# A scheduler rank 80 instructions ahead for the stages of neighbourhood attention and mLSTM

## The chip, the cores and the metric

The kernel runs on one core of a Trainium2 chip. The metric is device time in microseconds (us) of one launch, the median of several. TensorE does the matrix products and transposes, VectorE, ScalarE and GpSimd the arithmetic between them, and SyncE's queue issues the DMAs. In the profile they are PE (PEld is its weight load), DVE, ACT, POOL and SP.

## What is computed

Two models of two layers run one after the other on 512 tokens of 1024 features, in fp32. The first (two layers of sliding-window attention beside retention, then an MLP) takes up to about 1650 us and is not touched. The second has a context of 256 tokens beside x. Each of its layers, cut to what matters:

```python
h  = rmsnorm(x, g1) * (1 + sc1) + sh1          # adaLN: sh, sc, g from silu(c) @ w_ada
hc = the same for the context
p, pc = h @ w_in, hc @ w_in                    # q, k, v, o of mLSTM; q, k, v of attention; gates
# mLSTM, 8 heads of 64, both directions, context first, its end state begins x's scan
s   = (q @ k.T) * exp(b_t - b_s + i_s - m_t)
num = w_prev * (q @ C) + s @ v ;  den = w_prev * (q @ n) + sum(s)
y_m = head_layernorm(num / max(|den|, exp(-m_t))) * sigmoid(o)
# neighbourhood attention, 8 heads of 64, grid of 8 rows x 64 columns, 16 columns in sight
S   = [q @ k_window.T + bias + mask, q @ k_ctx.T]
y_n = softmax(S) @ [v_window, v_ctx]
x = x + g1 * ([y_m, y_n] @ w_out)
x = x + g2 * relu(modulated h @ w1)**2 @ w2    # the context too, but for the last layer
```

## The kernel before

Every large product is made of three fp32r products on TensorE: with a weight tile split in high and low parts (wh, wl) and the activation likewise, wh·xh, wh·xl, wl·xh (L241 to L243 where the weights are the loaded operand, L289 to L291 where they stream). Weights come by SyncE's DMA into wst (L215, 2 buffers); ScalarE makes whi (L225) and VectorE wlo (L226, the subtraction), 3 buffers each. PSUM has four tags: g with 3 buffers (products), s with 2 (scores), t with 2 (transposes, mLSTM states and outputs) and o with 1 (attention's values). SBUF tiles u come from one pool of 53.

*Neighbourhood attention of x* is na_x: 32 units, 8 heads by 4 blocks of 128 queries. Its stages: lead (once a head: key and query splits L405 to L422 on ScalarE and VectorE, 8 small bias DMAs L1286, 8 additions L1292 on GpSimd into btab); scores (products L1333 to L1339 into s; on VectorE the maxima L1341 and L1342, which adds the bias too, and the sign L1344; exp L1346 on ScalarE; then the division by the sum, L1220 and, by turns, L1222 on ScalarE or L1224 on VectorE); turn (transposes L1353 into t, copies L1355 and L1356); values (L1369 into o, every second head).

*mLSTM* is mlstm: 4 pairs of heads, each in steps of two chunks and two directions. Its stages: weights (row DMAs L1075, mask L1078 on GpSimd, exp L1081, and once a pair the turned keys, L1017 to L1023); prepare (row DMAs L1094, L1095 on VectorE, then the states: L1038 into t, VectorE's updates L1044); scores (L1106 into s, L1111 on VectorE); outs (L1118 and L1121 into t, the denominators L1123 to L1125, L1131 or L1134 on VectorE, the sum L1135 on GpSimd, and once a pair head_norm, L1159 to L1169); turn (L1145 into t, and a split L199 and L200).

Around them run the gate rows (scans L931 to L934 on VectorE), modulation for the next norms (products L824 into g, transposes L837 into t, sums L839 on VectorE), the rotations of q and k (L393 to L397, with swap DMAs L385) and the GEMMs. In order of time, second model: context mLSTM of layer 0 beside x's projections (1745 to 1870 us); x's attention beside more projections (to 2078); x's mLSTM beside the context's MLP (to 2300); x's MLP; then in layer 1 attention (2866 to 3014) and mLSTM (to 3200) beside what projections and modulation are left.

Two things set the order. First the program: generators are interleaved by mesh in proportion to their counts of steps, and within one, staged(n, *stages) runs in step i the stage d for unit i - d, deepest first, so that a stage that waits for another comes some steps later. Second, the scheduler below the program: it gives each instruction a rank, its place in the program, and lets each engine take next, of the instructions that are ready by its own reckoning, the one of lowest rank. Each engine then runs its list strictly as written. Buffers go round by tag in the order of the program.

Of the kernel before, what the change touches and what calls it, by code (L numbers as in the profile page):

```python
# [121 lines left out]
def staged(n, *stages):  # L122

    for i in range(n + len(stages) - 1):
        for d in reversed(range(len(stages))):
            if 0 <= i - d < n:
                stages[d](i - d)
        yield


def idle(i):
    pass


def chain(*gens):
# [14 lines left out]
class Net:  # L150
# [283 lines left out]
    def attention(self, zq, zk, av, sink8, ao):  # L434
# [57 lines left out]
        def values(i):  # L492
# [9 lines left out]
            if b == 3:  # L502
                ao.append(self.split(outs[p]))

        return staged(16, lead, idle, scores, idle, turn, idle, values)

    def retention(self, h, q, k, v, gate, rt):
# [72 lines left out]
    def first_block(self):  # L580
        nc, A = self.nc, self.A
        with self.pool("b1") as self.bp:
# [38 lines left out]

            nx, acc, hs = self.hybrid(0, acc, hs, gm, sink8[:, 0:8], chain([first], tiles), later)
            xs, acc, hs = self.hybrid(1, acc, hs, gm, sink8[:, 8:16], self.w_tiles(A["w_in"][1][:, 0:640], KT), idle)
        return xs, acc

# [177 lines left out]
    def modulation(self, l, i0, i1):  # L803
# [26 lines left out]
        def turn(i):  # L830
# [12 lines left out]
            if j in (3, 9):  # L843
# [4 lines left out]
                                               op0=ALU.add, op1=ALU.mult)  # L848

        return staged(i1 - i0, load, idle, work, turn)  # L850


# [201 lines left out]
    def mlstm(self, s, n, C, st, so, ys):  # L1054
# [7 lines left out]
        per = nch  # L1062
# [82 lines left out]
                nc.tensor.transpose(ps[:, 128 * c : 128 * c + 128], Hs[p][:, 128 * c : 128 * c + 128], self.ident)  # L1145
            ys.append(self.split(ps[:, :n], n))

        return staged(4 * per, weights, prepare, scores, idle, outs, idle, idle, turn)

    def head_norm(self, H, p, so, n):  # L1150

# [144 lines left out]
    def na_x(self, l, zq, zk, V, zkc, vc, ys):  # L1296

        nc = self.nc
        mm = nc.tensor.matmul
        grid = lambda ap: ap.rearrange("p (r c) -> p r c", c=64)  # L1300

        def perm(ap, out):
            if out:
                return ap.rearrange("p (b r c) -> p r b c", b=4, r=8)
            return ap.rearrange("p (r b c) -> p r b c", r=8, b=4)

        def patch(ap, v0, v1):

            ap = grid(ap)
            if v1 < 3:  # L1310
                return [(256, ap[:, :, 16 * v0 + 8 : 16 * v0 + 40].rearrange("p r (j c) -> p j r c", j=2))]
            outer = bass.AP(ap.tensor, ap.offset, [ap.ap[0], [56, 2], [64, 8], [1, 8]])
            return [(128, ap[:, :, 16 * v0 + 8 : 16 * v0 + 24]), (128, outer)]


        blocks = [(0, 0, 3), (256, 0, 1), (256, 1, 2), (512, 2, 3)]
        heads, outs, units = {}, {}, {}

        def lead(i):
            h, b = divmod(i, 4)  # L1320
            if b:
                return
            p, p0 = h // 2, 64 * (h % 2)
            heads[h] = (self.key_pairs(zk[p], p0, T), self.key_pairs(zkc[p], p0, 256),
                        self.query_stack(zq[p], p0, T, perm), self.bias_table(l, h))

        def scores(i):
            h, b = divmod(i, 4)
            o, v0, v1 = blocks[b]
            (kh, kl), (ch, cl), qs, tb = heads[h]  # L1330
            S = self.ps("s")
            lq = qs[:, 128 * b : 128 * b + 128]
            mm(out=S[:, 0:256], lhsT=lq, rhs=ch, start=True, stop=False)  # L1333
            mm(out=S[:, 0:256], lhsT=lq, rhs=cl, start=False, stop=True)
            mx, den = [self.t(self.bp, [128, 2], F32, tag, 4) for tag in ("nmx", "nden")]
            c = 256
            for (n, hi), (_, lo) in zip(patch(kh, v0, v1), patch(kl, v0, v1)):
                mm(out=S[:, c : c + n], lhsT=lq, rhs=hi, start=True, stop=False)
                mm(out=S[:, c : c + n], lhsT=lq, rhs=lo, start=False, stop=True)  # L1339
                c += n  # L1340
            nc.vector.tensor_reduce(mx[:, 0:1], S[:, 0:256], axis=AX.X, op=ALU.max)  # L1341
            nc.vector.tensor_tensor_reduce(S[:, 256:512], S[:, 256:512], tb[:, o : o + 256], 1.0, mx[:, 0:1],  # L1342
                                           ALU.add, ALU.max, mx[:, 1:2])
            nc.vector.tensor_scalar(mx[:, 1:2], mx[:, 1:2], -1.0, None, op0=ALU.mult)  # L1344
            P = units[i] = self.u()
            nc.scalar.activation(P, S, AF.Exp, bias=mx[:, 1:2], accum_out=den[:, 0:1])  # L1346
            self.na_scale(P, den[:, 0:1], i % 2)

        def turn(i):
            P = units[i]  # L1350
            pt = self.ps("t")
            for c in range(4):
                nc.tensor.transpose(pt[:, 128 * c : 128 * c + 128], P[:, 128 * c : 128 * c + 128], self.ident)  # L1353
            PT = units[i] = self.u()
            nc.scalar.activation(PT[:, 0:224], pt[:, 0:224], AF.Copy)  # L1355
            nc.vector.tensor_copy(PT[:, 224:512], pt[:, 224:512])  # L1356

        def values(i):
            h, b = divmod(i, 4)
            if h % 2 == 0:  # L1360
                return
            p = h // 2
            if b == 0:
                outs[p] = self.ps("o")
            PT = [units.pop(i - 4), units.pop(i)]
            _, v0, v1 = blocks[b]
            for c, v in enumerate((vc[0], vc[1], V[v0], V[v1])):
                for j in range(2):
                    mm(out=outs[p][64 * j : 64 * j + 64, 128 * b : 128 * b + 128],  # L1369
                       lhsT=v[:, 128 * p + 64 * j : 128 * p + 64 * j + 64], rhs=PT[j][:, 128 * c : 128 * c + 128],  # L1370
                       start=c == 0, stop=c == 3)
            if b == 3:
                self.na_finish(outs[p], T, perm, ys)

        return staged(32, lead, idle, idle, idle, idle, scores, idle, turn, idle, values)

    def na_values(self, w, hs, V, c0):

# [256 lines left out]
```

## Time and profile before

| | us |
|---|---|
| median of 3 runs | 3564.49 (3561.7 to 3566.58) |
| the profiled execution | 3575.06 |
| its span in the profile | 3573.3 |
| TensorE busy | 3437.6 (96%) |
| VectorE, ScalarE, GpSimd busy | 2023.8, 1444.9, 391.1 |

Busy time is that of one profiled execution, which took 10.6 us more than the median. TensorE's matmuls overlap and their ends are modelled, so 96% busy is not 96% of its peak; what TensorE waits for is read from its gaps and from the granted clock of a stretch.

### The profile page before, as it was taken

How to read it: one execution, taken by the hardware profiler on the slowest of the kernel's cores; microseconds unless marked ns; L12 is line 12 of the kernel's file. 1: busy time of each engine (PE TensorE's matmuls, PEld its weight loads, DVE VectorE, ACT ScalarE, POOL GpSimd, SP SyncE). 2: the span in 40 equal slices, each digit the busy share in tenths (PEclk: the TensorE clock that was granted, in tenths of full speed). 3: DMA queues.
4: the chain of work that ended last, by engine and by line, in shares of the span. 5: the costliest groups of instructions: out<-in, count | busy, mean ns of one | idle time of the engine just before them, and what ended most of it. 6: DMA issues, size and time to landing. Idle time of an engine off the chain costs nothing.

```text
span 3573.3 us, 48619 instructions
## 1 busy us (share of the span) xinstructions
PE 3437.6 (96%) x18835; PEld 2851.7 (80%) x18835; DVE 2023.8 (57%) x3791; ACT 1444.9 (40%) x2458; POOL 391.1 (11%) x512
## 2 busy tenths in 40 slices
PE   8999999999999999999998999999999999899998
PEld 7878888888778888787777788888888877668886
DVE  5654454455654454557657668764445577574444
ACT  4533332234532332335634664443334356333233
POOL 2120000001020010001112222100000122310000
PEclk9999999999999999999999999999999999899999
DMA  5322323334422432236645445533234334523322
GB/s 171 104 68 83 124 94 100 100 112 137 133 65 83 135 118 95 95 98 205 209 130 149 108 137 160 168 118 95 95 103 128 98 117 127 168 95 106 94 94 71
DMA packets 397655, 419.12 MB, mean 117 GB/s; under 512 B 38064, under 2 KB 343152, under 8 KB 397040
## 3 DMA queue, kind: packets, MB, share of 16 engines
q1 hardware_dynamic: 397424, 416.00, 37.4%
q8 instruction: 149, 2.44, 0.3%
q14 instruction: 82, 0.67, 0.1%
HBM read 391.55 MB, written 13.37 MB: 113 GB/s over the span
## 4 chain that ended last, share of the span: by engine, by line
PE 78%; DVE 9%; DMA 5%; ACT 3%; issue 3%; POOL 1%; SPq 1%; DVEq 0%; ACTq 0%; POOLq 0%
PE g L241 22%; PE g L242 22%; PE g L243 22%; DVE wlo L226 2%; PE g L289 1%; PE g L290 1%; PE g L824 1%; DMA u<-t 1%; PE g L291 1%; DMA u<-u 1%; ACT whi L225 1%; PE t L524 1%; DMA wst<-in_w_mlp 1%; PE o L1369 1%; POOL u L396 1%
## 5 line engine op out<-in xcount | busy, mean ns | idle before, releaser
L241 PE MATMUL g<-u,whi 128*128 128x512 f32 (+1 forms) x3680 | 1412.0, 384 | 9.5 <-ACT whi L225 3.1
L242 PE MATMUL g<-u,whi 128*128 128x512 f32 (+1 forms) x3680 | 1407.3, 383 | 4.9 <-DVE u L200 3.5
L243 PE MATMUL g<-u,wlo 128*128 128x512 f32 (+1 forms) x3680 | 1405.9, 382 | 3.4 <-DVE wlo L226 3.3
L225 ACT ACTIVATE whi<-wst 128x1024 fp32r<-128x1024 f32 (+1 forms) x628 | 621.7, 993 | 1352.2 <-PE g L242 1124.0
L226 DVE TENSOR_TENSOR wlo<-wst,whi 128x1024 fp32r<-128x1024 f32 (+1 forms) x628 | 729.0, 1164 | 425.4 <-ACT whi L225 417.7
L241 PEld LDWEIGHTS g<-u,whi 128*128 128x128 f32 x3680 | 694.8, 189 | 157.3 <-ACT whi L225 8.2
L242 PEld LDWEIGHTS g<-u,whi 128*128 128x128 f32 x3680 | 695.9, 189 | 138.3 <-DVE u L200 4.1
L243 PEld LDWEIGHTS g<-u,wlo 128*128 128x128 f32 x3680 | 694.9, 189 | 137.3 <-DVE wlo L226 5.5
L199 ACT ACTIVATE u<-u 128x512 fp32r<-128x512 f32 (+1 forms) x200 | 119.4, 597 | 289.7 <-DVE u L574 202.3
L200 DVE TENSOR_TENSOR u<-u,u 128x512 fp32r<-128x512 f32 (+1 forms) x200 | 132.9, 665 | 101.7 <-ACT u L199 100.9
L1485 DVE SCALAR_TENSOR_TENSOR u<-g,t,u 128x256 f32<-128x256 f32 (+1 forms) x128 | 78.1, 615 | 195.0 <-PE g L243 194.6
L289 PE MATMUL g<-whi,u 128*128 128x256 f32 (+1 forms) x576 | 167.9, 292 | 3.0 <-ACT rv L667 1.9
L291 PE MATMUL g<-whi,u 128*128 128x256 f32 (+1 forms) x576 | 164.6, 286 | 0.0
L290 PE MATMUL g<-wlo,u 128*128 128x256 f32 (+1 forms) x576 | 164.3, 286 | 0.0
L241 PE MATMUL g<-hc,whi 128*128 128x256 f32 x464 | 133.6, 290 | 6.9 <-ACT whi L225 5.1
L243 PE MATMUL g<-hc,wlo 128*128 128x256 f32 x464 | 132.0, 287 | 3.6 <-DVE wlo L226 3.6
L731 DVE TENSOR_TENSOR u<-g,u 128x512 f32<-128x512 f32 x64 | 44.3, 691 | 154.0 <-PE g L243 154.0
L242 PE MATMUL g<-hc,whi 128*128 128x256 f32 x464 | 131.3, 285 | 0.0
L868 POOL TENSOR_TENSOR u<-u,u 128x512 f32<-128x512 f32 (+1 forms) x28 | 35.7, 1274 | 864.4 <-ACT u L865 559.2
L289 PEld LDWEIGHTS g<-whi,u 128*128 128x128 f32 x576 | 110.7, 192 | 16.8 <-issue 7.7
L291 PEld LDWEIGHTS g<-whi,u 128*128 128x128 f32 x576 | 111.5, 193 | 1.2 <-issue 1.2
L290 PEld LDWEIGHTS g<-wlo,u 128*128 128x128 f32 x576 | 111.2, 193 | 1.1 <-issue 0.9
(302 smaller groups left out, 4055.4 us busy)
## 6 DMA issues: line engine op xcount, KB each, us to landing
wst<-in_w_mlp SPq DMA_DIRECT2D x96, 1024.0 KB, 5.4
wst<-in_w_in SPq DMA_DIRECT2D x60, 1024.0 KB, 5.4
u<-in_w_ada SPq DMA_DIRECT2D x192, 256.0 KB, 5.1
wst<-in_w_in SPq DMA_DIRECT2D x72, 512.0 KB, 4.0
wst<-in_w_up SPq DMA_DIRECT2D x32, 1024.0 KB, 5.5
wst<-in_w_down SPq DMA_DIRECT2D x32, 1024.0 KB, 5.2
wst<-in_w_out SPq DMA_DIRECT2D x20, 1024.0 KB, 5.4
u<-t SPq DMA_DIRECT2D x128, 128.0 KB, 5.2
```

The source lines that it names most:

```text
L199: nc.scalar.activation(hi, src, AF.Copy)
L200: nc.vector.tensor_tensor(lo, src, hi.bitcast(F32), op=ALU.subtract)
L225: nc.scalar.activation(h, v, AF.Copy)
L226: nc.vector.tensor_tensor(l, v, h.bitcast(F32), op=ALU.subtract)
L241: mm(out=ps, lhsT=wh, rhs=xh, start=first, stop=False)
L242: mm(out=ps, lhsT=wh, rhs=xl, start=False, stop=False)
L243: mm(out=ps, lhsT=wl, rhs=xh, start=False, stop=last)
L289: mm(out=ps, lhsT=xs[k][0][:, bs], rhs=wh[:, kk], start=k == 0, stop=False)
L290: mm(out=ps, lhsT=xs[k][0][:, bs], rhs=wl[:, kk], start=False, stop=False)
L291: mm(out=ps, lhsT=xs[k][1][:, bs], rhs=wh[:, kk], start=False, stop=k == KT - 1)
L731: nc.vector.tensor_tensor(t, ps, r2, op=ALU.mult)
L1485: V.scalar_tensor_tensor(xs[m], ps, mod[:, 40 + m, c : c + 1], xs[m], op0=ALU.mult, op1=ALU.add)
```

## The change

A helper, urgent, wraps the stages of mlstm and of na_x, so that whatever a stage emits gets a rank 80 places ahead of its place in the program. Idle stages stay as they are. The state-only mLSTM of the last layer's context (mlstm_states), the context's attention (na_ctx), GEMMs, gate rows, rotations and modulation are not wrapped. The order in which a stage takes its buffers is that of the program, as before. Each engine has the same instructions as before, in another order.

```diff
+def urgent(tc, ahead, *stages):
+
+    def wrap(f):
+        def g(i):
+            with tc.high_priority(ahead):
+                f(i)
+        return idle if f is idle else g
+    return [wrap(f) for f in stages]
...
-        return staged(4 * per, weights, prepare, scores, idle, outs, idle, idle, turn)
+        return staged(4 * per, *urgent(self.tc, 80, weights, prepare, scores, idle, outs, idle, idle, turn))
...
-        return staged(32, lead, idle, idle, idle, idle, scores, idle, turn, idle, values)
+        return staged(32, *urgent(self.tc, 80, lead, idle, idle, idle, idle, scores, idle, turn, idle, values))
```

The helper takes ten lines, so below it a line of the changed kernel has a number higher by 10: L1342 of before is L1352 there. A name such as s_2928 is a tile with its running number, the same in both.

VectorE in attention of layer 0, about 1936 to 1943 us in the trace, where s_2928 and s_2934 are the scores of two successive blocks, nmx their maxima, and u_2918 and u_2919 are gate rows. Before:

```order
L422 TENSOR_TENSOR u_2907_15776<-u_2772_15001,u_2907_15776 64x8x4x16
L931 SCALAR_TENSOR_TENSOR u_2918_15837<-u_2842_15456,mend_2411_13302,u_2841_15454 8x512
L932 SCALAR_TENSOR_TENSOR u_2918_15837<-u_2842_15456,mend_2411_13302,u_2841_15454 8x512
L1342 ISA s_2928_15868,nmx_2929_15871<-s_2928_15868,btab_2868_15583,nmx_2929_15871 128x256
L1342 ISA nmx_2929_15871 128x1
L933 SCALAR_TENSOR_TENSOR u_2919_15838<-u_2920_15841,u_2842_15456 8x512
L934 SCALAR_TENSOR_TENSOR u_2919_15838<-u_2920_15841,u_2842_15456 8x512
L1356 COPY u_2927_15865<-t_2926_15860 128x288
L1344 TENSOR_SCALAR nmx_2929_15871<-nmx_2929_15871 128x1
L1341 TENSOR_REDUCE nmx_2935_15895<-s_2934_15892 128x1
```

And changed:

```order
L1351 TENSOR_REDUCE nmx_2929_15871<-s_2928_15868 128x1
L1351 TENSOR_REDUCE nmx_2935_15895<-s_2934_15892 128x1
L1352 ISA s_2928_15868,nmx_2929_15871<-s_2928_15868,btab_2868_15583,nmx_2929_15871 128x256
L1352 ISA nmx_2929_15871 128x1
L1352 ISA s_2934_15892,nmx_2935_15895<-s_2934_15892,btab_2868_15583,nmx_2935_15895 128x256
L1352 ISA nmx_2935_15895 128x1
L1354 TENSOR_SCALAR nmx_2929_15871<-nmx_2929_15871 128x1
L405 TENSOR_TENSOR u_2890_15709<-u_2890_15709,u_2847_15466 128x512
L1354 TENSOR_SCALAR nmx_2935_15895<-nmx_2935_15895 128x1
L941 SCALAR_TENSOR_TENSOR u_2918_15837<-u_2842_15456,mend_2411_13302,u_2841_15454 8x512
L407 TENSOR_TENSOR u_2890_15709<-u_2890_15709,u_2891_15710 128x512
L942 SCALAR_TENSOR_TENSOR u_2918_15837<-u_2842_15456,mend_2411_13302,u_2841_15454 8x512
```

Both maxima, their bias additions and the sign of the first (L1344, now L1354) stand ahead of the gate scans and of the rotation L395 and L397 of u_2890 (now L405 and L407), which earlier stood ahead of L422 and after the first maximum.

TensorE at the same place, the scores s_2941 of the next block, before:

```order
L291 MATMUL g_2993_16194<-whi_2988_16184,u_2279_12684 128x256
L289 MATMUL g_2993_16194<-whi_2988_16184,u_2282_12716 128x256
L1333 MATMUL s_2941_15940<-u_2865_15566,u_2866_15571 128x256
L1334 MATMUL s_2941_15940<-u_2865_15566,u_2866_15571 128x256
L1338 MATMUL s_2941_15940<-u_2863_15560,u_2866_15571 128x256
L1339 MATMUL s_2941_15940<-u_2864_15561,u_2866_15571 128x256
L290 MATMUL g_2993_16194<-wlo_2989_16185,u_2282_12716 128x256
L291 MATMUL g_2993_16194<-whi_2988_16184,u_2283_12717 128x256
L289 MATMUL g_2993_16194<-whi_2988_16184,u_2290_12736 128x256
L290 MATMUL g_2993_16194<-wlo_2989_16185,u_2290_12736 128x256
L291 MATMUL g_2993_16194<-whi_2988_16184,u_2291_12737 128x256
L289 MATMUL g_2993_16194<-whi_2988_16184,u_2298_12776 128x256
```

And changed, up to the transposes t_2939 that need the first block's probabilities u_2931:

```order
L300 MATMUL g_2974_16096<-wlo_2913_15802,u_2298_12776 128x256
L1343 MATMUL s_2941_15940<-u_2865_15566,u_2866_15571 128x256
L1344 MATMUL s_2941_15940<-u_2865_15566,u_2866_15571 128x256
L1348 MATMUL s_2941_15940<-u_2863_15560,u_2866_15571 128x256
L1349 MATMUL s_2941_15940<-u_2864_15561,u_2866_15571 128x256
L301 MATMUL g_2974_16096<-whi_2912_15801,u_2299_12777 128x256
L299 MATMUL g_2974_16096<-whi_2915_15807,u_2301_12783 128x256
L300 MATMUL g_2974_16096<-wlo_2916_15808,u_2301_12783 128x256
L301 MATMUL g_2974_16096<-whi_2915_15807,u_2302_12784 128x256
L1343 MATMUL s_2952_16001<-u_2865_15566,u_2866_15571 128x256
L1344 MATMUL s_2952_16001<-u_2865_15566,u_2866_15571 128x256
L1363 MATMUL t_2939_15932<-t_35_36_104,u_2931_15880 128x128 x4
```

The scores now stand among the products of g_2974, which earlier were all ahead of them, and t_2939 follows after 4 more products and 2 of the scores of s_2952; before, it followed 8 products behind s_2941.

VectorE in the context mLSTM of layer 0, where t_2653 and t_2673 are outputs in PSUM, t_2665 and t_2666 sums for the states, and u_2655 the output that frees t_2653. Before:

```order
L1123 SCALAR_TENSOR_TENSOR mden_2654_14401<-t_2653_14394,gcols_2474_13555 128x4
L1044 SCALAR_TENSOR_TENSOR t_2209_2210_12343<-t_2209_2210_12343,wc_2480_13577,t_2665_14446 64x65
L1124 TENSOR_TENSOR mden_2654_14401<-mden_2654_14401,t_2653_14394 128x4
L1044 SCALAR_TENSOR_TENSOR t_2209_2210_12343<-t_2209_2210_12343,wc_2480_13577,t_2665_14446 64x65
L1125 RECIPROCAL mden_2654_14401<-mden_2654_14401 128x4
L1044 SCALAR_TENSOR_TENSOR C_2588_14061<-t_2209_2210_12343,wc_2480_13577,t_2665_14446 64x65 x2
L1134 TENSOR_TENSOR u_2655_14405<-t_2653_14394,mden_2654_14401 128x256
L1044 SCALAR_TENSOR_TENSOR t_2209_2210_12343<-t_2209_2210_12343,wc_2480_13577,t_2666_14457 64x65
```

And changed, the rows up to the same u_2655:

```order
L1054 SCALAR_TENSOR_TENSOR C_2588_14061<-t_2209_2210_12343,wc_2480_13577,t_2666_14457 64x65 x2
L236 TENSOR_TENSOR wlo_2670_14477<-wst_2668_14474,whi_2669_14476 128x1024
L1133 SCALAR_TENSOR_TENSOR mden_2674_14516<-t_2673_14509,gcols_2474_13555 128x4
L236 TENSOR_TENSOR wlo_2691_14570<-wst_2668_14474,whi_2690_14569 128x1024
L1134 TENSOR_TENSOR mden_2674_14516<-mden_2674_14516,t_2673_14509 128x4
L1135 RECIPROCAL mden_2674_14516<-mden_2674_14516 128x4
L236 TENSOR_TENSOR wlo_2720_14726<-wst_2718_14723,whi_2719_14725 128x1024
L1144 TENSOR_TENSOR u_2655_14405<-t_2653_14394,mden_2654_14401 128x256
```

Three weight splits (L226, now L236) and the denominators of the next output t_2673 came between the denominators of t_2653 and u_2655.

## Rows read from the trace of the kernel before

**Rows 1.** the page's head and first part: busy time of each engine
```profile
span 3573.3 us, 48619 instructions
...
PE 3437.6 (96%) x18835; PEld 2851.7 (80%) x18835; DVE 2023.8 (57%) x3791; ACT 1444.9 (40%) x2458; POOL 391.1 (11%) x512
```

**Rows 2.** stretches A:B: length, then busy us (instructions) by engine, PE clock granted
```profile
1745.00:1870.00 125.00, 121.28 (x746) 94.98 (x746) 69.22 (x204) 52.91 (x104) 26.80 (x46) 0.97 0.51 161
1870.00:2078.00 208.00, 190.20 (x1348) 158.80 (x1348) 145.33 (x342) 119.62 (x230) 54.34 (x95) 0.95 0.43 121
2078.00:2300.00 222.00, 204.73 (x1735) 195.45 (x1732) 185.54 (x434) 113.34 (x231) 52.42 (x67) 0.96 0.52 159
2866.00:3014.00 148.00, 138.86 (x939) 113.11 (x938) 119.33 (x282) 83.14 (x175) 37.86 (x60) 0.99 0.39 112
3014.00:3200.00 186.00, 163.02 (x1022) 119.18 (x1021) 114.74 (x318) 75.32 (x152) 47.79 (x62) 0.88 0.47 149
sum 889.00, PE 818.09 PEld 681.52 DVE 634.16 ACT 444.33 POOL 219.20; mean PE 163.62 PEld 136.30 DVE 126.83 ACT 88.87 POOL 43.84
```

**Rows 3.** what ended TensorE's waits, 1870 to 2078: us, times, longest
```profile
PE t L1353 <- DVE u L1224: 5.4, 3, 2.3
PE s L1333 <- ACT u L1346: 4.5, 2, 4.2
...
PE t L1353 <- ACT u L1222: 2.1, 2, 1.7
```

**Rows 4.** TensorE in order of time: start, us, [idle before <-what ended it]
```profile
1939.69 0.28 PE L291 MATMUL g<-whi,u 128*128 128x256 f32 x1
1939.80 0.28 PE L289 MATMUL g<-whi,u 128*128 128x256 f32 x1
1944.30 0.58 PE L1333 MATMUL s<-u,u 128*128 128x256 f32 x1 [4.22 <-ACT u L1346]
```

**Rows 5.** ScalarE in order of time, the exp before those scores
```profile
1943.47 0.69 ACT L1346 ACTIVATE u<-s,nmx 128x512 f32<-128x512 f32 x1 [4.11 <-DVE nmx L1344]
```

**Rows 6.** VectorE in order of time, the same place
```profile
1934.33 0.69 DVE L397 TENSOR_TENSOR u<-u,u 128x512 f32<-128x512 f32 x1 [1.74 <-POOL u L396]
...
1937.22 1.27 DVE L931 TENSOR_TENSOR_SCAN u<-u,mend,u 8x512 f32<-8x512 f32 x1
...
1939.81 0.49 DVE L1342 CUSTOM_DVE_ANT_0 s<-s,btab,nmx 128x256 f32<-128x256 f32 x1
...
1941.55 1.21 DVE L934 TENSOR_TENSOR_SCAN u<-u,u 8x512 f32<-8x512 f32 x1
...
1943.28 0.15 DVE L1344 TENSOR_SCALAR nmx<-nmx 128x1 f32<-128x1 f32 x1
```

**Rows 7.** two half-clock stretches, columns as in rows 2
```profile
1941.00:1947.80 6.80, 3.50 (x17) 3.50 (x17) 6.59 (x20) 2.08 (x6) 0.09 (x1) 0.61 0.48 155
3099.00:3115.00 16.00, 13.69 (x39) 7.30 (x38) 9.12 (x27) 2.76 (x7) 0.23 (x1) 0.52 0.26 78
```

**Rows 8.** VectorE's larger weight splits, 2078 to 2300: count, busy us, mean ns
```profile
L226 DVE TENSOR_TENSOR wlo<-wst,whi 128x1024 fp32r<-128x1024 f32 x27 | 32.7, 1219 | 14.1 <-ACT whi L225 13.9 <-issue 0.3
```

**Rows 9.** what ended TensorE's waits, 1745 to 1870
```profile
PE t L1038 <- DVE u L1134: 2.3, 1, 2.3
```

**Rows 10.** what ended TensorE's waits, 2078 to 2300
```profile
PE g L243 <- DVE wlo L226: 5.3, 6, 1.7
```

**Rows 11.** line L226 alone, 2078 to 2300: count, ns min/median/max
```profile
L226 DVE TENSOR_TENSOR wlo<-wst,whi x81: 677/693/1759, 2077.0 to 2299.2; 128x512 fp32r<-128x512 f32 x54, 128x1024 fp32r<-128x1024 f32 x27
```

**Rows 12.** what ended TensorE's waits, 2866 to 3014
```profile
PE s L1333 <- ACT u L1346: 2.2, 2, 2.0
...
PE o L1369 <- DVE u L1356: 1.4, 2, 1.2
```

**Rows 13.** what ended TensorE's waits, 3014 to 3175
```profile
PE t L837 <- DVE u L1356: 3.4, 1, 3.4
```

**Rows 14.** what ended the waits of SyncE's queue, 1745 to 2300
```profile
SPq L215 <- DVE wlo L226: 112.5, 18, 16.9
```

## The prediction

> **What bounds the kernel now.** I read the page first: TensorE is busy 3437.6 of 3573.3 us, 96% [rows 1]. Nothing but its own work, its waits and its clock can move the end by much, and the change takes no work away: each engine keeps every instruction that it had. So I went to TensorE's idle and half-clock time. The order is the same on every engine up to about 1750 us of the span, and nearly the same between 2300 and 2866 us, where only x's MLP runs; neither part can change by itself. The table by stretches [rows 2] gives the rest: 889 us in which TensorE is busy 818, so 71 us are idle (about 65 of them in gaps over 0.15 us). The granted clock there is 0.88 to 0.99 of full, which is a few stretches at half speed (1.2 GHz for 2.4) among full-speed ones. These two stocks, 71 us of idling and the half-clock time, are all that a new order can gain from. What it can lose is not bounded so: it can make new waits.
>
> Then I asked for each of these stretches what ended TensorE's waits, and laid out the work queued on each engine in the old and the new order, each instruction with its own duration from the trace; "earlier by 5 us" below means that so much less work stands ahead of it on its own engine.
>
> **The change, part by part.** In these five stretches a stage of attention or mLSTM moves ahead of up to 80 instructions (over all engines) of the surrounding GEMMs, of modulation and of the gate arithmetic. Nothing is added.
>
> *Attention, layer 0 (1870 to 2078 us).* TensorE waits 4.5 us for exp, 5.4 us for the scaled probabilities (L1224) and 2.1 us for those of ScalarE (L1222) [rows 3]. The largest single wait is 4.22 us, for scores s_2941 [rows 4]. It needs the s buffer that exp frees; exp waited 4.11 us for the negated maximum L1344 [rows 5]; and on VectorE the maximum L1342 of that block stands behind L397 with its 1.74 us wait and two gate scans, and L1344 behind two scans more [rows 6]. Scans L931 to L934 take 1.27, 1.27, 1.21 and 1.21 us. With L397 (0.69 + 1.74) that is 7.4 us of queue; the new order puts all of it behind L1344, and the next block's L1341 and L1342 (some 0.9 us) ahead: exp can start about 6.5 us sooner. TensorE also comes to s_2941 sooner, as 13 of the 24 products of g_2974 that stood ahead go behind it, at 0.11 us each (the step between rows at full clock [rows 4]), 1.4 us. That wait nearly vanishes. But next come the transposes L1353 t_2939, which need P after L1224, and on VectorE the delayed work now stands there: L395 (0.7, as L397), L397, L931, L932, two copies L1356 and L1224 (0.5 each) and two small ones, 5.6 us after the L1344 in question. Exp (0.7 [rows 5] and 0.2 to read its sum), scores and the 4 products left between them give TensorE about 2.3 us of that. So about 3.3 us of the 4.2 come back as a wait of L1353 for L1224, and with its remainder at s_2941 I take 0 for this place. Bounds: the whole 4.2 us goes, and the half-clock stretch after it (3.50 us busy at 0.61 [rows 7], so 3.50 x 0.39 = 1.4 us), -5.6; the scans cost a second such wait, +3. Near 2012 us, transposes t_3130, which waited 1.7 us for L1222, get 23 products ahead, 23 x 0.11 = 2.5 us, which covers them: -1.7 (0 to -1.7). The other attention scores there move up by 1 to 2 us, transposes by none, so L1224's 5.4 us stand, neither gain nor loss.
>
> *Context mLSTM, layer 0 (1745 to 1870 us).* Scores come 5 to 7 us earlier on TensorE, outs 4 to 6 us; both had 9 us and more to spare in the trace, so that is worth nothing by itself. The t tag of PSUM has two buffers, and states (L1038) and outs (L1118) take them in turn; L1134 frees the one of outs. In the old order VectorE reaches L1134 of u_2655 right behind the reciprocal and two state updates. In the new one three weight splits of 128x1024 stand ahead (1.22 us each [rows 8]), with products L1123 that wait for TensorE. The one L1038 that waited for L1134 paid 2.3 us [rows 9]. By the queues, two more states and one outs now come 4.6 to 7 us before their buffer is free, of which the GEMM products behind cannot help, since TensorE takes its work in order; part is the same wait seen three times. I take one and a half waits of the old size more: +3.5 (0 to +7).
>
> *mLSTM of x, layer 0 (2078 to 2300 us).* Scores move up 10 us and outs 6 us, from 18 us and more of slack: 0. What is passed is the weight splits L226, 1.4 us later at the median and up to 9.9. TensorE's products by wlo already wait for them 6 times, 5.3 us [rows 10]: here there is no slack, VectorE being busy 186 of 222 us [rows 2]. With three wlo buffers most of the delay is absorbed; I take half the old wait again: +2.5 (-2 to +8: the longest of them gone at one end; at the other each doubled, and 3 us for a half-clock stretch).
>
> One rule speaks against the change in these first three stretches. VectorE's splits meet GpSimd work: of 81 splits the median takes 0.69 us and the longest 1.76 [rows 11]. The Trainium skill, page "SBUF — State Buffer", section "Summary: rules for kernel authors", says that a VectorE operation with two SBUF inputs and a GpSimd operation that reads SBUF exclude each other, the later one blocking until the first ends. The slow splits of this trace agree with that, though no run here isolates it. By it, if GpSimd's bias and state work drawn forward met each of the six waiting splits, at 0.5 us each, the sum would be some 3 us higher, 3568.
>
> *Attention, layer 1 (2866 to 3014 us).* The same change of scans against L1342. TensorE waits 2.2 us for exp and 1.4 us for copies L1356 [rows 12], both behind scans. Scores move up 3 us and their products by V 4 us, with producers that hardly move. Of the 3.6 us I take half away: -2 (-5 with the other short waits, +3 if the lead of 3 us becomes a wait).
>
> *mLSTM of x, layer 1 (3014 to 3200 us).* Here TensorE is busy 163 of 186 at 0.88 [rows 2], the worst stretch; 3099 to 3115 alone lost 13.69 x 0.48 = 6.6 us to the clock [rows 7], and L837 waits 3.4 us for a t buffer that L1356 frees [rows 13]. But little GEMM work is left to overtake, the shifts are 0 to 3 us, and the chain of t buffers stays: -2 (-8, that clock and half of that wait; +4, one more such wait).
>
> *SyncE's queue.* Bias loads (8 per head) and row loads L1075 go ahead of some weight loads and swaps L385. Weight loads L215 stood waiting for a split to free their buffer, 18 times, 112.5 us [rows 14], so a place in the queue is not what sets them: 0, at most +3 (half of the mean wait of 6 us, once).
>
> Sum: 0 - 1.7 + 3.5 + 2.5 - 2 - 2 + 0 = +0.3 us on the profiled run's 3575.06 us. That run is 10.6 us above the median 3564.49, 1.8 us of it outside the span; I put the sum on the median: 3564.8. The ends added up are -22 and +28, but they are not one event.
>
> **The rivals.** *A, faster: GEMM work saved becomes filler.* The products passed over are still there when the latency chains at the end of each stretch run dry, so later gaps and half-clock stretches close as well. For it: the scores move by more than their waits. Against it: the transposes, the next link, don't move. If half of 12.0 us [rows 3], 3.6 [rows 12], 3.4 [rows 13] and 1.4 + 6.6 of clock [rows 7] go, that is 13.5 us, and no new waits come: 3551. All of it would be 3537.
>
> *B, slower: weight splits come late.* Attention and mLSTM fill VectorE ahead of L226, and TensorE stands at the third product of a tile with nothing behind that it may do first. For it: the six waits without slack; against it: three buffers. With context +7, mLSTM +8, L1353 +3 and the gains -5: +13, 3577. It decides from the point where the delay of a split (median 1.4 us) exceeds what its buffers hold in hand.
>
> *C: the order changes and the time of no wait does*, because TensorE reaches its data later than it is made, or the producers on ScalarE and VectorE set each step: 3564.5. It lies inside my forecast, and I count it there.
>
> **How the numbers follow.** About 0.2%, 7 us, is what a measurement of this kernel can tell from no change, so 3557.4 to 3571.6 is "the same". Forecast with C 0.46, spread 3556 to 3572: 0.42 inside, 0.04 below. A 0.29, faster. B 0.25, slower. Faster 0.33, same 0.42, slower 0.25. A reaches down to 3537 and B to about 3583; of each I leave out the far third, 0.17 in all: 3545 to 3578. The forecast's own range is 3556 to 3572.
>
> **What would show it.** Right: the 4.2 us wait of L1333 for exp is gone and a wait of L1353 for L1224 or L1220 of 2 to 4 us stands near it; L1038 and L1118 wait in all 3 to 7 us between 1745 and 1870; waits of L243 for wlo rise from 5.3 to about 8 us in the mLSTM of layer 0; the stretch up to 1745 us is as long as before. Wrong towards A: idle time over the affected stretches falls below 60 us, the clock in the tail above 0.92. Wrong towards B: L243 for wlo above 12 us, new half-clock stretches between 2078 and 2300.

## The result and the profile after

| | before | after |
|---|---|---|
| median, us | 3565.53 (4 runs, 3561.7 to 3568.41) | 3594.31 (4 runs, 3590.1 to 3599.64) |
| profiled execution, us | 3575.06 | 3593.33 |
| its span, us | 3573.3 | 3591.5 |
| TensorE busy, us | 3437.6 | 3463.2 |

The ratio of after to before is 1.0074, with a 95% interval of 1.0055 to 1.0093: the change costs about 27 us. The prediction was 3564.8 with a range of 3545 to 3578, so it was wrong. The profiled run of before stood 10 us above its median and that of after at its median, so the two traces show only 18 us of the difference.

The head of the page after:

```profile
span 3591.5 us, 48655 instructions
...
PE 3463.2 (96%) x18835; PEld 2853.2 (79%) x18835; DVE 2024.0 (56%) x3791; ACT 1443.9 (40%) x2458; POOL 385.4 (11%) x512
```

Against [rows 1], TensorE is busy 25.6 us longer with the same 18835 products; VectorE and ScalarE work as long as before, GpSimd 5.7 us less. The table by stretches, with the columns of [rows 2], each stretch moved by what the work had slipped at its ends:

```profile
1745.00:1869.00 124.00, 122.62 (x747) 93.82 (x746) 68.42 (x205) 53.43 (x104) 26.67 (x46) 1.00 0.52 163
1869.00:2080.00 211.00, 199.03 (x1345) 158.46 (x1344) 146.46 (x342) 118.61 (x229) 50.43 (x94) 0.96 0.44 124
2080.00:2310.00 230.00, 211.57 (x1707) 198.73 (x1706) 179.84 (x427) 110.41 (x228) 51.11 (x67) 0.95 0.51 154
2876.00:3034.00 158.00, 148.60 (x931) 114.27 (x931) 116.90 (x280) 81.95 (x172) 36.45 (x60) 0.99 0.36 103
3034.00:3218.00 184.00, 162.72 (x1023) 118.88 (x1022) 116.67 (x316) 76.69 (x155) 48.52 (x62) 0.91 0.49 152
sum 907.00, PE 844.55 PEld 684.15 DVE 628.29 ACT 441.10 POOL 213.18; mean PE 168.91 PEld 136.83 DVE 125.66 ACT 88.22 POOL 42.64
```

The reading takes two subtractions. Idle time of TensorE *fell*, from 889 - 818 = 71 us to 907 - 844.6 = 62 us. The granted clock of TensorE is no worse in sum (0.97 to 1.00 in the first stretch, 0.96 to 0.95 in the third, 0.88 to 0.91 in the last). Both stocks that the prediction watched moved the right way, and yet the stretches take 18 us longer, because TensorE's own work grew by 26.5 us. Attention of layer 0 (208 to 211 us), mLSTM of layer 0 (222 to 230) and attention of layer 1 (148 to 158) lost; the context mLSTM (125 to 124) and the last mLSTM (186 to 184) did not.

Which products grew is seen when the page's groups are asked for by line, from 1745 us to the end of the affected part. The columns are busy us and mean ns of one, then idle time before. Before:

```profile
L1369 PE MATMUL o<-u,u 128*64 128x128 f32 x256 | 30.7, 292 | 1.4 <-DVE u L1356 1.4
...
L1369 PE MATMUL o<-u,hc 128*64 128x128 f32 x256 | 23.8, 275 | 0.0
...
L1106 PE MATMUL s<-u,u 64*128 64x128 f32 x160 | 22.0, 335 | 1.0 <-DVE u L1111 0.5 <-ACT u L1346 0.5
```

And after:

```profile
L1379 PE MATMUL o<-u,u 128*64 128x128 f32 x256 | 43.4, 300 | 3.8 <-DVE u L1366 2.2 <-DVE u L1225 1.4 <-ACT u L1365 0.2
...
L1379 PE MATMUL o<-u,hc 128*64 128x128 f32 x256 | 32.9, 294 | 0.0
...
L1116 PE MATMUL s<-u,u 64*128 64x128 f32 x160 | 30.2, 339 | 2.1 <-DVE u L1121 1.1 <-ACT u L1356 1.0
```

Attention's values grew from 54.5 to 76.3 us and mLSTM's scores from 22.0 to 30.2, at nearly the same mean per product. Busy time counts the time in which at least one product of the group runs, so the products that share this time have become fewer: many that ran two at a time before run one at a time now. Both groups use half of the array: 128*64 is 64 columns (the two heads of a pair beside each other), 64*128 is 64 rows. The order in time shows how. TensorE before, one block of values (columns: start, us, line):

```profile
2004.38 0.66 PE L1369 MATMUL o<-u,u 128*64 128x128 f32 x8
2004.87 0.61 PE L1369 MATMUL o<-u,hc 128*64 128x128 f32 x8
```

Eight products (an fp32 product leaves two records) run through in 1.1 us. TensorE after, two score products of one block, then a block of values of the same kind as above:

```profile
1960.31 0.28 PE L1348 MATMUL s<-u,u 128*128 128x256 f32 x1
1960.43 0.29 PE L1349 MATMUL s<-u,u 128*128 128x256 f32 x1
...
1961.68 0.38 PE L1343 MATMUL s<-u,u 128*128 128x256 f32 x1
1961.99 0.43 PE L1379 MATMUL o<-u,u 128*64 128x128 f32 x2
1962.35 0.66 PE L1363 MATMUL t<-t,u 128*128 128x128 f32 x4
1962.94 0.43 PE L1379 MATMUL o<-u,u 128*64 128x128 f32 x2
1963.30 0.39 PE L1344 MATMUL s<-u,u 128*128 128x256 f32 x1
1963.62 0.43 PE L1379 MATMUL o<-u,u 128*64 128x128 f32 x2
1963.98 0.33 PE L1348 MATMUL s<-u,u 128*128 128x128 f32 x1
```

Single value products stand between single score products and transposes. From start to start a lone value product takes 0.36 us (1961.99 to 1962.35) and a score product 0.31 (1961.68 to 1961.99), where a score product inside its own block steps by 0.12 (1960.31 to 1960.43). Nothing waits here: the rows carry no idle time. The order pieces ahead of the prediction showed scores among GEMM products, but not this.

### The profile page after: what moved, and what is told of

Read it like the earlier page. It is cut to its first block, busy times and chain, and to the rows that moved or that the text cites. A ratio compares the mean times of both kernels' runs of the same rounds, so it can differ in the third digit from the quotient of the medians.

```text
span 3591.5 us, 48655 instructions
## 1 busy us (share of the span) xinstructions
PE 3463.2 (96%) x18835; PEld 2853.2 (79%) x18835; DVE 2024.0 (56%) x3791; ACT 1443.9 (40%) x2458; POOL 385.4 (11%) x512
## 4 chain that ended last, share of the span: by engine, by line
PE 81%; DVE 9%; ACT 3%; DMA 3%; issue 2%; POOL 1%; SPq 1%; DVEq 0%; POOLq 0%; ACTq 0%
PE g L251 22%; PE g L253 22%; PE g L252 22%; DVE wlo L236 2%; PE g L299 1%; PE g L300 1%; PE g L301 1%; PE g L834 1%; PE o L1379 1%; DMA u<-u 1%; PE t L534 1%; ACT whi L235 1%; PE t L1131 1%; PE t L1363 1%; POOL u L406 1%
## 5 line engine op out<-in xcount | busy, mean ns | idle before, releaser
L253 PE MATMUL g<-u,wlo 128*128 128x512 f32 (+1 forms) x3680 | 1405.7, 383 | 4.2 <-DVE wlo L236 3.7
L236 DVE TENSOR_TENSOR wlo<-wst,whi 128x1024 fp32r<-128x1024 f32 (+1 forms) x628 | 725.7, 1158 | 430.9 <-ACT whi L235 423.1
L253 PEld LDWEIGHTS g<-u,wlo 128*128 128x128 f32 x3680 | 693.2, 189 | 139.6 <-DVE wlo L236 7.1
L253 PE MATMUL g<-hc,wlo 128*128 128x256 f32 x464 | 133.0, 289 | 0.6 <-DVE wlo L236 0.5
```

The source lines that it names most:

```text
L236: nc.vector.tensor_tensor(l, v, h.bitcast(F32), op=ALU.subtract)
L253: mm(out=ps, lhsT=wl, rhs=xh, start=False, stop=last)
```

## The experiments

Two theories were open at first. **S**: TensorE pays for a change between fp32 products and fp32r products (fp32r is the format of the large products). **B**, the prediction's rival: weight splits come late on VectorE. S was replaced by **T** after price, ahead20, ahead160 and glue_after: TensorE pays for a change between products on the full array and on half of it, and a half-array product without its partner runs alone. The counts are taken from the program's order on TensorE, over the whole kernel. A change is counted wherever one product and the next use different shapes of the array: 128x128, 64 columns, 64 rows, or the 32 columns of modulation's products (L824); the expectations call all of these changes between full-array and half-array products. A product on part of the array is alone when neither neighbour uses the same shape at another place of the array.

| kernel | changes of shape | alone | ratio to before, 95% interval | median, us |
|---|---|---|---|---|
| before | 432 | 92 | | 3565 to 3570 |
| after | 591 | 163 | 1.0074 (1.0055 to 1.0093) | 3594.3 |
| ahead20 | 758 | 271 | 1.0151 (1.0134 to 1.0168) | 3618.1 |
| ahead160 | 570 | 163 | 1.0110 (1.0095 to 1.0125) | 3605.2 |
| glue_after | 486 | 110 | 1.0047 (1.0032 to 1.0062) | 3583.5 |
| rev_after | 385 | 84 | 0.9980 (0.9970 to 0.9991) | 3561.8 |
| vrev_before | 387 | 72 | 0.9957 (0.9943 to 0.9970) | 3553.4 |
| na_only | 539 | 120 | 1.0029 (1.0014 to 1.0043) | 3573.3 |
| ml_only | 464 | 127 | 1.0033 (1.0022 to 1.0044) | 3578.1 |
| rev_before | 374 | 69 | 0.9953 (0.9937 to 0.9968) | 3549.5 |
| few_changes | 284 | 54 | 0.9948 (0.9928 to 0.9968) | 3547.4 |

The kernels were timed in groups, each beside its own runs of before: to glue_after (3565.4; after itself 3565.5), rev_after and vrev_before (3570.1), and the rest (3565.3). Between groups the ratios are to be compared, not the medians.

**price: what a change of number format costs.** The added products, at the end:

```diff
+        for i in range(96):
+            mm(out=g[:, 0:256], lhsT=r[:, 128:256], rhs=r[:, 0:256], start=True, stop=True)
+        for i in range(96):
+            mm(out=t[:, 0:128], lhsT=f[:, 128:256], rhs=f[:, 0:128], start=True, stop=True)
+        for i in range(96):
+            one_r(i)
+            one_f(i)
```

> The kernel before with 864 products added behind its last output, which no output depends on: 192 fp32r products of 128x256 (192 in a row, the first 96 to warm the clock), 96 fp32 products of 128x128 in a row, then 96 of each by turns, then 24 times four of one and four of the other, then 96 fp32r again. Theory S (TensorE pays for each change between fp32 and fp32r products): from the trace of before and after, a change there and back costs about 0.22 us, so the part by turns takes 96 x 0.22 = 21 us longer than the two rows of 96 together, the part by fours 24 x 0.22 = 5 us longer. Rival B (nothing is paid for a change, the loss comes from weight splits that come late): both parts take as long as the two rows together, within 1 us.

TensorE in order of time, the two rows of 96 and the first rounds by turns:

```profile
3573.48 11.68 PE L794 MATMUL g<-u 128*128 128x256 f32 x96
3585.01 21.60 PE L796 MATMUL t<-u 128*128 128x128 f32 x192
3606.36 0.36 PE L786 MATMUL g<-u 128*128 128x256 f32 x1
3606.57 0.38 PE L789 MATMUL t<-u 128*128 128x128 f32 x2
3606.70 0.36 PE L786 MATMUL g<-u 128*128 128x256 f32 x1
```

In rows, an fp32r product takes 11.5 / 96 = 0.12 us and an fp32 product 21.4 / 96 = 0.22. By turns a round takes 0.34 (3606.36 to 3606.70), the sum of the two. A change of format costs nothing, and by fours neither (24 rounds from 3639.00 to 3671.80, 32.8 us). S falls.

**ahead20, ahead160, glue_after.** The first two change one number, in both return lines; the third keeps a block's products together:

```diff
-        return staged(32, *urgent(self.tc, 80, lead, ...
+        return staged(32, *urgent(self.tc, 20, lead, ...
```

```diff
+    def glue(self, on):
+        import contextlib
+        return self.tc.high_priority(2000) if on else contextlib.nullcontext()
...
             for c, v in enumerate((vc[0], vc[1], V[v0], V[v1])):
                 for j in range(2):
-                    mm(out=outs[p][64 * j : 64 * j + 64, ...
+                    with self.glue(c or j):
+                        mm(out=outs[p][64 * j : 64 * j + 64, ...
```

> The change with 20 in place of 80. Changes between fp32 and fp32r products on TensorE, counted in the order: 744 before, 960 with 80, 1258 with 20. Weight splits on VectorE stand 0.4 us later in the mean in the mLSTM of layer 0, against 2.2 with 80. Theory S (each change costs about 0.11 us): 514 changes more than before, +57 us, 3622, some 30 us slower than with 80. Rival B (late weight splits): the delay is a fifth of that with 80, so between before and after, 3566 to 3575.

> The change with 160 in place of 80. Changes between fp32 and fp32r products: 932 (960 with 80). Weight splits in the mLSTM of layer 0 2.8 us later in the mean (2.2 with 80). Theory S: 188 changes more than before, +21 us, 3587, a little faster than with 80. Rival B: slower than with 80, about 3600.

> The change as it is, but in each stage the products on TensorE after the first of a block (scores, transposes, outs, states, values) get a rank 2000 places ahead, so that a block that has begun is not cut up. Changes between fp32 and fp32r products: 804 (744 before, 960 after). Weight splits in the mLSTM of layer 0 stand 2.5 us later in the mean (2.2 after): VectorE's order is that of after. Theory S: 60 changes more than before, +7 us, 3572. Rival B: as after, 3594 or more.

ahead20 came to 3618.1 (S said 3622, B at most 3575): with hardly any delay of the weight splits (0.4 us in the mean) it is the worst of all, so B can't be the main cause. Its rows by line, columns as above:

```profile
L1379 PE MATMUL o<-u,u 128*64 128x128 f32 x256 | 45.7, 298 | 0.7 <-DVE u L1366 0.4 <-ACT u L1365 0.2
L1379 PE MATMUL o<-u,hc 128*64 128x128 f32 x256 | 37.8, 291 | 0.0
L1048 PE MATMUL t<-vw,u 128*64 128x65 f32 x384 | 34.9, 243 | 1.8 <-DVE hrs L327 1.7
```

The states L1038 (L1048 here), 18.4 us before, are the third group on half of the array, and now they are cut as well. glue_after missed S's 3572 by 11 us and was 11 us better than after: keeping blocks whole helped by less than hoped, because it did not keep the values whole. The order shows 84 runs of value products in it, 114 after and 54 before, for 32 blocks; the first product of a block needs only the copy L1355 and went ahead, and the others waited for L1356. ahead160 was 18 us above S's figure and near B's, slower than after with fewer changes. Its trace shows where: TensorE's work at full clock (added up as described under price2) is 6 us less than after's, as the counts ask, but TensorE spent 110 us of its busy time at half clock, against 74 after, which costs 18. Why the clock fell there more often wasn't tried.

**price2: what a change of the array's tiling costs.**

```diff
+        for i in range(48):
+            cols(0), cols(1)
+        for i in range(48):
+            cols(0)
...
+        for i in range(48):
+            full(), cols(0), cols(1)
...
+        for i in range(48):
+            full(), cols(0), full(), cols(1)
```

> The kernel before with rows of products added behind its last output, which no output depends on: full-array products (fp32r 128x256, or fp32 128x128), pairs of products that each use 64 columns of the array (fp32, 128 columns wide, as the values of attention) and pairs that use 64 rows each (as the scores of mLSTM), each alone in a row and by turns. Theory T (TensorE pays for each change between a product on the full array and one on half of it, and a half-array product that stands without its partner runs alone): full, pair, full, pair takes 0.3 to 0.5 us a round longer than the same products in rows; a pair split by a full product costs more than twice that round; the change costs as much with fp32 full-array products as with fp32r. Rival S (the change between fp32 and fp32r is what costs; the first price run speaks against it): fp32 full products with fp32 pairs by turns cost nothing extra. Rival B: no row by turns costs more than its parts.

TensorE in order of time, pairs and singles in rows (48 pairs and 48 alone), a full row, then full products and pairs by turns:

```profile
3590.01 21.18 PE L792 MATMUL o<-u 128*64 128x128 f32 x288
3611.11 11.90 PE L786 MATMUL g<-u 128*128 128x256 f32 x97
3622.94 0.44 PE L792 MATMUL o<-u 128*64 128x128 f32 x4
3623.31 0.39 PE L786 MATMUL g<-u 128*128 128x256 f32 x1
3623.62 0.44 PE L792 MATMUL o<-u 128*64 128x128 f32 x4
```

A pair takes 0.22 us in a row (48 pairs, 3590.0 to 3600.5), and so does one of its products alone (48, to 3611.1). Full and pair by turns take 0.69 a round (3622.94 to 3623.62 and on; 48 rounds) where 0.12 + 0.22 = 0.34 is their sum: **0.35 us for there and back.** Later in the same trace, a pair split by full products:

```profile
3667.38 0.43 PE L792 MATMUL o<-u 128*64 128x128 f32 x2
3667.75 0.39 PE L786 MATMUL g<-u 128*128 128x256 f32 x1
3668.06 0.43 PE L792 MATMUL o<-u 128*64 128x128 f32 x2
```

0.68 us for a full product and half a pair, so 1.36 for the split pair with two full ones, against 0.46 in rows: 0.90 us more, where the whole pair costs 0.35. With fp32 full products the round with a pair is 0.79 against 0.44; with pairs on 64 rows 0.74 against 0.34; with four full products and two pairs 1.25 against 0.92. So going to half the array and back costs 0.33 to 0.40 us in each of these rounds, in both formats and both lengths tried: T holds, in the size that it gave (0.3 to 0.5).

The Trainium skill states the rule, in "TensorEngine Tiling (Array Packing)", section "Key Properties": changing the tiling mode, not just the tile, drains TensorE. These runs agree and give the price here, 0.35 us there and back. I had not weighed that page; it speaks against the change.

A pair of 0.22 us is 0.11 for each product, so a product alone costs 0.11 more. By T's prices after should cost 159 / 2 x 0.35 + 71 x 0.11 = 36 us at full clock. Added up from start to start in the traces (gaps left out, half-clock time counted half), TensorE's work over the second model's attention and mLSTM grew by 39.5 us; idle time and half-clock time fell by 9 and 12 us. 39.5 - 9 - 12 is the 18 us of the traces. The 12 us of clock belong mostly to before's profiled execution, which stood 10 us above its median: in eight of the ten other kernels of the table the trace loses 8 to 14 us less to the clock than before's. Between medians, then, some 27 of the 39.5 us arrive. That longer work on TensorE fills some of its waits fits the 9 us of idle time; no run separates it from what the new order does to the waits.

**rev_after and vrev_before: the cuts repaired.**

```diff
-            for c, v in enumerate((vc[0], vc[1], V[v0], V[v1])):
-                for j in range(2):
+            vs = (vc[0], vc[1], V[v0], V[v1])
+            for c in (3, 2, 1, 0):
+                for j in (1, 0):
```

> As glue_after, and the products of attention's values in reverse order of the four value blocks, so that the first waits for the copy that comes last and the rest follow it without a break. Changes between full-array and half-array products on TensorE, counted in the order: 432 before, 591 after, 486 in glue_after, 385 here. Weight splits stand as late as in glue_after. Theory T (0.24 us a change, from the trace: time of TensorE's work at full clock against these counts in four kernels): 101 changes fewer than glue_after, 24 us less: 3559. Rival B (late weight splits): as glue_after, 3583, or slower.

> The kernel before, with only the reverse order of the value products: no rank is changed and no weight split stands later by more than 1 us in the stretches up to 3014 us. Changes between full-array and half-array products: 387 against 432. Theory T: 45 fewer, 11 us less, 3554. Rival B: 3565, as before.

Against its own runs of before rev_after is 7 us faster (T asked for 6) and vrev_before 15 (T 11); B has both wrong. rev_after keeps the change's ranks and its late weight splits and is by the ratios 24 us faster than glue_after, slightly faster than before. vrev_before touches no rank at all, and that edit alone gives 15 us. Its values, in the columns above (54.5 us before):

```profile
L1370 PE MATMUL o<-u,hc 128*64 128x128 f32 x256 | 22.2, 295 | 3.1 <-DVE u L1356 3.0
L1370 PE MATMUL o<-u,u 128*64 128x128 f32 x256 | 20.1, 280 | 0.0
```

**na_only and ml_only: which half of the change.** One of the two return lines stays as before.

> The change for attention's stages alone. Changes between full-array and half-array products on TensorE: 539 (432 before, 591 after); half-array products without their partner: 120 (92 before, 163 after). Weight splits in the mLSTM of layer 0 stand no later than before. Theory T, now with the prices of the second price run (0.35 us for there and back, 0.11 us for a product alone): 107 / 2 x 0.35 + 28 x 0.11 = +22 us at full clock, 3588, some us less where waits close. Rival B (late weight splits, which are worst in the mLSTM of layer 0): at most +5.

> The change for mLSTM's stages alone. Changes between full-array and half-array products: 464; products without their partner: 127. Weight splits in the mLSTM of layer 0 as late as after (2.2 us in the mean). Theory T: 32 / 2 x 0.35 + 35 x 0.11 = +9.5 us, 3575. Rival B: +20 or more, most of the loss of after.

na_only costs 10 us, ml_only 12, in sum 22 of the 27. Neither is the time that T forecast. In the trace of na_only TensorE's work grew by the 22 us that T asks for, but its idle time fell by 11. In that of ml_only work grew by 18 us, twice T's 9.5; B's 20 or more is no better, since the waits of L253 for wlo are no longer than before (5.6 us from 1745 to 3250, L243's were 6.9). The groups fall apart cleanly. na_only, values and then mLSTM scores:

```profile
L1379 PE MATMUL o<-u,u 128*64 128x128 f32 x256 | 44.1, 306 | 6.0 <-DVE u L1366 4.5 <-DVE u L1225 1.3 <-ACT u L1365 0.2
L1379 PE MATMUL o<-u,hc 128*64 128x128 f32 x256 | 32.2, 300 | 0.0
L1116 PE MATMUL s<-u,u 64*128 64x128 f32 x160 | 19.4, 321 | 2.5 <-ACT u L1356 1.5 <-DVE u L1121 1.0
```

And ml_only, the same groups in the order of its view:

```profile
L1379 PE MATMUL o<-u,u 128*64 128x128 f32 x256 | 30.8, 289 | 1.5 <-DVE u L1366 1.5
L1116 PE MATMUL s<-u,u 64*128 64x128 f32 x160 | 28.7, 327 | 2.0 <-DVE u L1121 1.3 <-ACT u L1356 0.5
L1379 PE MATMUL o<-u,hc 128*64 128x128 f32 x256 | 23.9, 275 | 0.0
```

Of these two groups attention's urgency cuts only the values, mLSTM's only the scores.

**rev_before and few_changes: a version that beats both.** rev_before is rev_after without urgent. few_changes adds more uses of glue and this:

```diff
+            if b % 4 != 4 - 1:
+                return
...
+            for d in range(4):
+                PT = [units.pop(i - d - 4), units.pop(i - d)]
```

> The kernel before with the two remedies of rev_after (blocks kept whole by rank, value products in reverse order) and no stage moved ahead by 80. Changes between full-array and half-array products: 374 (385 in rev_after, 387 in vrev_before). Theory T: 58 fewer than before, 29 x 0.35 = 10 us, and 23 products fewer alone, 2.5 us: 3553. If the ranks of the change cost something beside the cuts, this is faster than rev_after by more than 2 us; if keeping blocks whole by rank costs it, it is slower than vrev_before.

> rev_before, and the values of attention done for four blocks of queries in a row, and the blocks of modulation, of the context's attention and of the first model's values kept whole by rank as well. Changes between full-array and half-array products: 284 (432 before); without a partner 54 (92). Theory T: 148 / 2 x 0.35 + 38 x 0.11 = 30 us less than before, 3536, less what waiting for four blocks adds. Rival B: no faster than vrev_before, 3553.

rev_before came to 3549.5 (T 3553), by the ratios 10 us faster than rev_after with nearly as many changes (374 and 385): the ranks cost something beside the cuts, and T explains 4 us of it. few_changes, 3547.4 (T 3536), is no different from rev_before by its interval. TensorE's work fell by a further 14 us, nearly all of it in modulation, whose blocks on 32 columns it keeps whole: that line is busy 68.5 us in the whole of rev_before and 53.1 here. But idle time rose by 10 us, before transposes and scores; that values of four blocks in a row come late for what waits on them is likely, but not shown. Both are about 0.5% faster than before.

Added up as under price2, but over the whole kernel, TensorE's work at full clock differs from before's by 39, 71, 32, 20, -2, -12, 22, 18, -19 and -33 us in the order of the table from after on; T's prices give 36, 77, 32, 11, -9, -10, 22, 9, -13 and -30. So T gives the work of each kernel within 9 us. In glue_after, rev_after and ml_only, all with mLSTM's ranks moved, 7 to 9 us more stand than it asks for, and in na_only none; but after, ahead20 and ahead160, which move them too, lie at 3, -6 and 0, so this explains nothing yet.

## Why the prediction was wrong

**The step that failed is the first.** "The change takes no work away: each engine keeps every instruction that it had", and so I looked only at idle time and clock, as if the products had a price of their own. They don't: those on half of the array cost by their neighbours. The two stocks that I added up moved by 9 us of idle time and 12 of clock, both gains; the loss of 39.5 us of work at full clock was in no term and in no rival. Rival B had the direction, slower, but its mechanism did not come. None of the signs that I named looked at TensorE's busy time: those towards A were just missed (62 us of idle time, a clock of 0.91), and of those towards B the waits of L243 for wlo stood at 3.7 us of 12, while the clock in that stretch only went from 0.96 to 0.95.

**Attention, layer 0: the place was right.** The wait of 4.22 us at s_2941 [rows 4] became three. TensorE after, in order of time:

```profile
1939.92 0.58 PE L1343 MATMUL s<-u,u 128*128 128x256 f32 x1 [2.76 <-ACT u L1356]
...
1942.29 0.58 PE L1343 MATMUL s<-u,u 128*128 128x256 f32 x1 [0.29 <-ACT u L1356]
...
1944.22 0.69 PE L1363 MATMUL t<-t,u 128*128 128x128 f32 x2 [1.13 <-DVE u L1234]
```

2.76 + 0.29 + 1.13 = 4.18 us: a term of 0, as forecast, but partly by luck, since the split between the two was the other way (I had the wait at s_2941 nearly gone and 3.3 us at L1353). Over the stretch, waits for exp, L1224 and L1222 [rows 3] fell from 12.0 to 6.2 us:

```profile
PE s L1343 <- ACT u L1356: 3.4, 3, 2.8
PE t L1363 <- DVE u L1234: 2.4, 2, 1.3
...
PE t L1363 <- ACT u L1232: 0.4, 2, 0.2
```

The 2.1 us for L1222, with the 1.7 near 2012, became 0.4, as forecast; the 5.4 for L1224, which I left standing, became 2.4. So waits did close, as in rival A, by some 6 us; but TensorE's busy time in the same stretch rose by 8.8 (190.2 to 199.0).

**Context mLSTM: wrong in sign.** I gave +3.5 us for waits of t buffers. After, no L1038 waits there at all, and the longest wait is of another line:

```profile
PE t L1407 <- DVE u L1141: 1.0, 1, 1.0
```

The stretch is 1 us shorter, with the clock up from 0.97 to 1.00. The buffers that by the queues came free late made no wait; the runs don't show why.

**mLSTM of layer 0, rival B: mis-sized.** I gave +2.5 for weight splits. Waits of L243 for wlo went from 5.3 [rows 10] to:

```profile
PE g L253 <- DVE wlo L236: 3.7, 7, 0.8
```

So the delay, 2.2 us in the mean, did not lengthen these waits; that the three buffers absorbed it is the likely reason. The stretch still lost 8 us, 6.8 of them in TensorE's busy time. ahead20, slowest with the least delay, and rev_after, faster than before with the whole delay, show that the delay of the splits is not what costs.

**Attention, layer 1:** -2 expected, +10 measured. Waits for exp barely moved from the 2.2 us of [rows 12], and TensorE's busy time rose by 9.7 us:

```profile
PE s L1343 <- ACT u L1356: 2.1, 2, 1.5
```

**mLSTM of layer 1:** -2 expected, -2 measured, which is luck. L837's wait of 3.4 us for L1356 is gone, but in its place L1048 waits 2.8 us for L1144 and L1379 2.2 for L1366. TensorE's work at full clock rose by 5 us, and the clock, up from 0.88 to 0.91, paid for it.

The Trainium skill's rule on GpSimd and VectorE that I weighed ("SBUF — State Buffer", "Summary: rules for kernel authors") would have raised the sum by 3 us. VectorE's busy time was 2023.8 and 2024.0 us, so the runs show none of it.

**What stays open.** By the ratios rev_after is 10 us slower than rev_before at nearly equal counts, so some 10 of the change's 27 us remain where both sides have their cuts repaired. In these two traces TensorE's work differs by about 16 us: 4 in modulation, 3 in mLSTM's scores, the rest spread over the GEMM products, and no run tells why. Nor is it known why ahead160 lost more to the clock. The counts explain the direction of every kernel and TensorE's work within 9 us, but not each time within 10 us.

## What to carry to other kernels

Before you move work in an engine's order, ask whether its price depends on its neighbours: on TensorE here, each stretch of products on half the array costs about 0.35 us for entering and leaving, and a product without its partner takes as long as the two together. Count these runs in the order of both programs, which needs no chip; in this kernel it told, against before, whether each experiment would be faster or slower. When a block is cut, look at which of its inputs arrives last: starting the block with the product that needs that input kept it whole, and was worth 15 us, where every change of ranks alone made the kernel slower than before.

## What was not expected of the hardware

Switching by turns between fp32 and fp32r products on the full array costs nothing (0.34 us a round, the sum of 0.12 and 0.22). A half-array product on 64 columns alone takes as long as its pair (0.22 us). Going to products on half the array and back costs 0.33 to 0.35 us with 64 columns and 0.40 with 64 rows. And TensorE's idle share was no measure of the loss: the kernel with the least idle time in the stretches, ahead20, is the slowest.
